# Second layer's feed-forward input projection by seven block products instead of eight (Strassen's method), its sums on GpSimd

## The chip, the cores and the metric

The kernel runs on one core of a Trainium2 chip. A core has five engines with an instruction queue each: TensorE (PE, matrix products, with its weight loads as PEld), VectorE (DVE), ScalarE (ACT), GpSimd (POOL) and SyncE (SP, which issues DMAs here). Each engine runs its own list in a fixed order, and engines wait for each other by semaphores. SBUF is the on-chip memory of 128 partitions, PSUM the accumulators of TensorE in eight banks. The metric is device time in microseconds of one execution: before, the median of three runs is 2463.46 us (2461.73, 2463.46, 2464.15).

## The reference, cut to what matters

A step of a two-layer backbone on 640 tokens (128 context tokens, 512 latent tokens), model width 1024, feed-forward width 2816. Each layer has mixers (convolution, recurrence, attention), an output projection with a gated residual, and then the feed-forward part, which is what is changed, in layer index 1 alone:

```
def trunk_layer(x, cvec, l, rope, ctx, params):
    ...
    x = x + g1 * (m @ w_out[l])
    h2 = rmsnorm(x, norm2[l]) * (1 + sc2) + sh2
    gu = h2 @ w_ffn_in[l]                       # 1024 -> 2 * 2816
    ff = jax.nn.silu(gu[..., :D_FF]) * gu[..., D_FF:]
    x = x + g2 * (ff @ w_ffn_out[l])
```

Everything is float32. `sc2`, `sh2`, `g2` come from the conditioning and differ between context and latent tokens.

## The kernel before, in words

Activations lie transposed: channels on the 128 partitions (1024 channels are 8 chunks `k`), the 640 tokens in the columns. TensorE takes float32 products as three passes of a shorter form (`fp32r`): each operand is a high part plus a low part, and a product is hi·hi + hi·lo + lo·hi. So `gemm` (its matmul is L301) makes one 128-row tile of an output with 8 k × 3 matmuls for each of two token halves, `HALF` = 256 and 384 columns: 48 matmuls a tile.

**Weights.** `panel8` brings a panel of 128 × 2048 raw float32 into one of two `rawt` buffers (one DMA of 1024 KB); for the feed-forward input (`wfi`) it holds 8 k × (128 gate columns | 128 up columns). `split_cols` makes the two parts of a tile in the ring `wR` (three slots of 1024 columns, high and low): L271 on ScalarE casts the high part, L272 on VectorE subtracts it from the raw weights for the low part.

**Activations.** Before the feed-forward part `accumulate_last` runs the last output projection of the layer with both token halves apart: first half of all eight tiles, then second half. Behind each half `after` calls `make_h`, which needs the token sums of squares of that half (`SqSum`, L504 and L505), their reciprocal root (a chain of small VectorE operations, L337 to L354), and then makes `hR_f` chunk by chunk: L521 on VectorE, L522 on ScalarE (high part), L523 on VectorE (low part).

**Feed-forward.** 22 panels stand in groups `FF_GROUPS` of 4, 2, 4, 4, 4, 4. A panel is two tiles, gate and up: 96 matmuls. The gate's eviction (`ev_silu2`) is L611 on ScalarE (tanh) and L612 on VectorE; the up tile is multiplied in by L1398 on VectorE, and `split_act` (L287 on ScalarE, L288 on VectorE) puts the high and low part into `oR`. Behind each group `accumulate` runs the output projection of that group's channels (`wfo`, matmuls L301 on `oR`) and adds into `xt` with L1187 on VectorE. The first two panels of the first group run with their first token halves ahead of their second ones (`run_tiles(jobs[:2], True)`), so that the second half of `make_h` has time.

**What sets the order.** A scheduler lays down each engine's list before the run from priorities: an instruction gets a running number, and instructions in `hp()` one that is 20000 smaller, so that they go as early as their inputs allow. Loads, splits of weights and evictions are in `hp()`. GpSimd does nothing but memsets.

Of the kernel before, what the change touches and what calls it, by code (L numbers as in the profile page):

```python
# [39 lines left out]
class Arena:  # L40
# [58 lines left out]
def tile_trunk_step(  # L99
# [55 lines left out]
    class Scope:  # L155


        def __init__(self, name, side):
            self.stack = ExitStack()
            self.name = name  # L160
            self.pool = self.stack.enter_context(tc.tile_pool(name=name, bufs=1, side=side, reuse_waits="tile"))
# [65 lines left out]
    def hp():  # L227
        return prio(20000)
# [32 lines left out]
    def split_cols(raw3):  # L261

        K, c = raw3.shape[1], raw3.shape[2]
        if wx:
            parts = [r.ap[:, : K * c] for r in wx.pop()]
        else:
            ctr["wr"] += 1
            parts = [wR[:, ctr["wr"] % NW, i, : K * c] for i in range(2)]
        hi, lo = [x.rearrange("p (k c) -> p k c", k=K) for x in parts]
        with hp():  # L270
            S.copy(hi, raw3)  # L271
            V.tensor_tensor(out=lo, in0=raw3, in1=f32(hi), op=ALU.subtract)  # L272
        return [(hi[:, k], lo[:, k]) for k in range(K)]
# [16 lines left out]
    def sub(wk, c):  # L290
        return [(h[:, c * P : (c + 1) * P], l[:, c * P : (c + 1) * P]) for h, l in wk]

    def gemm(wk, ak, hf):

        sl = HALF[hf]
# [49 lines left out]
    def stat_rstd(s, sl, scale, eps, post=None, ring=None):  # L345


        pair = (ring or wring).next()
        n = (sl.stop - sl.start) // P
        for i in range(n):  # L350
            T.matmul(pair[:, 0, i * 64 : (i + 1) * 64], lhsT=s[:, sl.start + i * P : sl.start + (i + 1) * P], rhs=ones[:, :64], start=True, stop=True)  # L351
        var = small(n)
        src = pair[:, 0, : n * 64].rearrange("p (i e) -> p i e", e=64)[:, :, 0]
        V.tensor_scalar(out=var, in0=src, scalar1=scale, scalar2=eps, op0=ALU.mult, op1=ALU.add)  # L354
        r = small(n)
        rsqrt(r, var, n)
# [123 lines left out]
    def open_h(name):  # L480
        sc = Scope(name, "left")
        hR = sc.tile([P, 2, KD, NT], F32R, "hR")
        h_act[:] = [(hR[:, 0, k, :], hR[:, 1, k, :]) for k in range(KD)]
        return sc
# [4 lines left out]
        return sc  # L489

    class SqSum:
        def __init__(self, ring, s):
            self.s = s
            self.n = [0, 0]
            self.ring = ring

        def add(self, src, hf):
            sl = HALF[hf]
            n = sl.stop - sl.start
            if self.n[hf] == 0:  # L500
                S.activation(self.s[:, sl], src[:, sl], AF.Square)
            else:
                sq = self.ring()
                S.activation(sq[:, :n], src[:, sl], AF.Square)  # L504
                V.tensor_tensor(out=self.s[:, sl], in0=self.s[:, sl], in1=sq[:, :n], op=ALU.add)  # L505
            self.n[hf] += 1

    def make_h(xs, sq, l, which, hf):

        sc = modd[l][:, 0 if which == 0 else 2]  # L510
        sh = modt[l][:, 0:8] if which == 0 else modt[l][:, 24:32]
        sl = HALF[hf]
        with hp():
            pb = stat_rstd(sq.s, sl, 1.0 / 1024, 1e-6)
        for j in range(KD):
            t = next_t()[:, : sl.stop - sl.start]
            hi, lo = h_act[j]
            for s, ss in streams(sl):
                tt = t[:, ss.start - sl.start : ss.stop - sl.start]
                pp = pb[:, ss.start - sl.start : ss.stop - sl.start]  # L520
                V.scalar_tensor_tensor(out=tt, in0=xs[j][:, ss], scalar=sc[:, j, s : s + 1], in1=pp, op0=ALU.mult, op1=ALU.mult)  # L521
                S.activation(hi[:, ss], tt, AF.Identity, bias=sh[:, j, s : s + 1])  # L522
                last = V.scalar_tensor_tensor(out=lo[:, ss], in0=tt, scalar=sh[:, j, s : s + 1], in1=f32(hi[:, ss]), op0=ALU.add, op1=ALU.subtract)  # L523
        return last
# [595 lines left out]
    def acts(lst):  # L1120
        return [(hi.ap, lo.ap) for hi, lo in lst]
# [76 lines left out]
                if j % every == every - 1:  # L1198
                    behind(last, other, 1)

    def accumulate_last(load, ak, xs, g, after):

        with four_slots():
            tiles = load(0) + load(1)
            for hf in range(2):
                for j, wk in enumerate(tiles):
                    ps, sl = gemm(wk, ak, hf)
# [35 lines left out]
    for l in range(DEPTH):  # L1243
# [77 lines left out]
        left = open_h(f"f{l}")  # L1321
# [12 lines left out]
        def out_panel(k, n):  # L1334
            return lambda pn: panel_wide(wout[l, :, k : k + n, 512 * pn : 512 * (pn + 1)], n)
# [26 lines left out]
        accumulate_last(out_panel(4, 4), acts([mh[j] for j in range(4, 8)]), xr, G1, after)  # L1362
        free_all([mh[j] for j in range(4, 8)])
        ssq.free()

        mods = iter(())
        if l + 1 < DEPTH:
# [156 lines left out]
```

## Time and profile before

| | |
|---|---|
| median of three runs | 2463.46 us |
| the profiled execution, whole | 2464.25 us |
| its span, first to last instruction | 2462.3 us |
| TensorE busy | 2429.8 us (99%) |
| VectorE busy | 1741.5 us (71%) |
| ScalarE busy | 911.1 us (37%) |
| GpSimd busy | 3.2 us |
| granted TensorE clock, mean | 0.995 |

The span is the time in which the profile saw instructions, and the whole execution is 1.95 us longer. An engine's busy time is the sum over its instructions. Lines (L301) are those of the kernel's code; "out<-in" are the program's names. A group of matmuls in the timeline carries the shape of its first one.

### The profile page before, as it was taken

What the parts mean: (1) busy time and instruction counts of PE and PEld (TensorE: products, weight loads), DVE (VectorE), ACT (ScalarE), POOL (GpSimd) and SP (SyncE); (2) the same over time, 40 slices, a digit from 0 to 9 for tenths busy, and PEclk for the clock granted to TensorE, in tenths of its full rate; (3) what the DMA queues carried; (4) which work ended last, traced back from release to release, by engine and by line L of the source; (5) the groups of instructions that cost most, each with busy time, mean ns of one, the idle gap of its engine ahead of it and who ended that gap; (6) DMA issues with size and microseconds to landing.
All of it is one profiled execution on the core that took longest, in us unless ns stands there. A gap on an engine that the chain in (4) does not pass through costs nothing.

```text
span 2462.3 us, 41375 instructions
## 1 busy us (share of the span) xinstructions
PE 2429.8 (99%) x17054; PEld 2374.3 (96%) x17054; DVE 1741.5 (71%) x3570; ACT 911.1 (37%) x1741; POOL 3.2 (0%) x36
## 2 busy tenths in 40 slices
PE   6999999999999999999999999999999999999999
PEld 4999999899999999999999999999999999999999
DVE  8588898676768897767785879977566874444343
ACT  6244664544323412222242446644333241222221
POOL 0000000000000000000000000000000000000000
PEclk8999999999999999999999999999999999999999
DMA  7122212333252244334332221121222412212121
GB/s 275 66 81 103 84 52 83 132 115 124 76 182 93 103 172 159 132 136 155 127 116 71 99 93 69 52 71 67 82 87 62 163 67 69 86 69 86 69 77 69
DMA packets 60493, 251.01 MB, mean 102 GB/s; under 512 B 6416, under 2 KB 18448, under 8 KB 37776
## 3 DMA queue, kind: packets, MB, share of 16 engines
q1 hardware_dynamic: 60304, 248.37, 28.9%
q8 instruction: 134, 2.20, 0.4%
q14 instruction: 55, 0.45, 0.1%
HBM read 230.52 MB, written 17.83 MB: 101 GB/s over the span
## 4 chain that ended last, share of the span: by engine, by line
PE 92%; DVE 5%; ACT 1%; issue 1%; DMA 0%; SPq 0%; DVEq 0%; ACTq 0%
PE psum L301 74%; PE psum L312 8%; PE psum L823 3%; PE psum L402 1%; PE psum L1074 1%; DVE aF_b L684 1%; DVE wR L272 1%; DVE small L1044 1%; PE psum L864 1%; PE psum L1066 1%; PE psum L1037 1%; PE psum L1038 1%; ACT wR L271 0%; PE psum L879 0%; PE psum L351 0%
## 5 line engine op out<-in xcount | busy, mean ns | idle before, releaser
L301 PE MATMUL psum<-hR_a,wR 128*128 128x256 f32 (+1 forms) x4512 | 705.3, 312 | 0.0
L301 PEld LDWEIGHTS psum<-hR_a,wR 128*128 128x128 f32 x4512 | 666.0, 189 | 3.0 <-issue 0.2
L271 ACT CAST wR<-rawt 128x1024 fp32r<-128x1024 f32 x316 | 329.8, 1049 | 796.9 <-PE psum L301 761.5
L272 DVE TENSOR_TENSOR wR<-rawt,wR 128x1024 fp32r<-128x1024 f32 x316 | 384.9, 1222 | 324.3 <-ACT wR L271 323.5
L301 PE MATMUL psum<-hR_f,wR 128*128 128x256 f32 (+1 forms) x4128 | 609.7, 309 | 0.0
L301 PEld LDWEIGHTS psum<-hR_f,wR 128*128 128x128 f32 x4128 | 604.1, 188 | 0.0
L301 PE MATMUL psum<-oR,wR 128*128 128x384 f32 (+1 forms) x3840 | 584.6, 311 | 4.1 <-DVE xt_x L1187 3.7
L301 PEld LDWEIGHTS psum<-oR,wR 128*128 128x128 f32 x3840 | 566.8, 190 | 8.0 <-DVE xt_x L1187 5.1
L1187 DVE SCALAR_TENSOR_TENSOR xt_x<-psum,modd,xt_x 128x128 f32<-128x128 f32 (+1 forms) x432 | 173.5, 436 | 109.7 <-PE psum L301 102.5
L312 PE MATMUL psum<-wR,hR_a 128*128 128x256 f32 x1920 | 235.2, 281 | 0.0
L312 PEld LDWEIGHTS psum<-wR,hR_a 128*128 128x128 f32 x1920 | 228.6, 188 | 0.7
L684 DVE SCALAR_TENSOR_TENSOR aF_b<-aF_b,pk 128x655 f32<-128x655 f32 x240 | 214.9, 895 | 2.8
L444 DVE CUSTOM_DVE_ANT_0 aF_m<-aF_m 128x1024 f32<-128x1024 f32 x112 | 136.7, 1220 | 0.8
L1398 DVE TENSOR_TENSOR ur<-ur,psum 128x256 f32<-128x256 f32 (+1 forms) x88 | 42.9, 488 | 74.9 <-PE psum L301 74.7
L287 ACT CAST oR<-ur 128x256 fp32r<-128x256 f32 (+2 forms) x96 | 45.8, 479 | 89.8 <-DVE ur L1398 81.3
L611 ACT ACTIVATE ur<-psum 128x256 f32<-128x256 f32 (+1 forms) x104 | 45.3, 435 | 75.4 <-PE psum L301 75.4
L1044 DVE TENSOR_REDUCE small<-psum 128x1 f32<-128x640 f32 (+1 forms) x80 | 55.1, 710 | 24.1 <-PE psum L1038 20.8
L823 PE MATMUL psum<-aF_b 128*128 128x128 f32 x500 | 70.4, 289 | 0.1
L823 PEld LDWEIGHTS psum<-aF_b 128*128 128x128 f32 x500 | 64.6, 192 | 3.7 <-issue 0.7
L811 ACT COPY aF_b<-aF_b 128x640 f32<-128x640 f32 x50 | 39.4, 787 | 75.8 <-DVE aF_b L827 40.8
L1047 ACT ACTIVATE aX<-psum,small 128x640 f32<-128x640 f32 (+1 forms) x80 | 56.5, 710 | 23.3 <-DVE small L1045 23.2
L612 DVE SCALAR_TENSOR_TENSOR ur<-ur,psum 128x256 f32<-128x256 f32 (+1 forms) x104 | 50.3, 484 | 19.2 <-ACT ur L611 19.1
(200 smaller groups left out, 2005.1 us busy)
## 6 DMA issues: line engine op xcount, KB each, us to landing
rawt<-in_win_dram SPq DMA_DIRECT2D x64, 1024.0 KB, 4.8
rawt<-in_wfi_dram SPq DMA_DIRECT2D x44, 1024.0 KB, 4.7
aF_m<-in_wmodT_dram SPq DMA_DIRECT2D x28, 1024.0 KB, 4.8
rawt<-in_wfo_dram SPq DMA_DIRECT2D x20, 1024.0 KB, 4.9
rawt<-in_wmod_dram SPq DMA_DIRECT2D x12, 1024.0 KB, 4.8
rawt<-in_wbr_dram SPq DMA_DIRECT2D x24, 512.0 KB, 3.3
aF_b<-in_wmod_dram SPq DMA_DIRECT2D x8, 1024.0 KB, 9.9
gd<-ur SPq DMA_DIRECT2D x16, 320.0 KB, 2.1
```

The lines of the kernel that those rows point to most:

```text
L271: S.copy(hi, raw3)
L272: V.tensor_tensor(out=lo, in0=raw3, in1=f32(hi), op=ALU.subtract)
L287: S.copy(hi, src)
L301: T.matmul(ps, lhsT=w, rhs=a[:, sl], start=k == 0 and q == 0, stop=k == n - 1 and q == 2)
L312: T.matmul(ps, lhsT=a[:, sl], rhs=w, start=k == 0 and q == 0, stop=k == n - 1 and q == 2)
L444: V.tensor_tensor_reduce(out=out, in0=w[:, q * 1024 : (q + 1) * 1024], in1=cb[s], scale=1.0, scalar=0.0, op0=ALU.mult, op1=ALU.add, accum_ ...
L612: V.scalar_tensor_tensor(out=dst[:, sl], in0=dst[:, sl], scalar=1.0, in1=ps, op0=ALU.add, op1=ALU.mult)
L684: V.scalar_tensor_tensor(out=accs[j], in0=pads[j][:, t : t + CO], scalar=w(j, t), in1=accs[j], op0=ALU.mult, op1=ALU.add)
L823: T.matmul(ps[:, c // 4, (c % 4) * P : (c % 4 + 1) * P], lhsT=kc[:, c * P : (c + 1) * P], rhs=qm[:, c * nc1 : (c + 1) * nc1], start=True, ...
L1044: V.tensor_reduce(out=mx[:, c : c + 1], in_=srcs[c], axis=AX.XY, op=ALU.max)
L1047: S.activation(e.rearrange("p (h n) -> p h n", h=2 if i else 1), srcs[c], AF.Exp, bias=mx[:, c : c + 1], scale=0.125, accum_out=sm[:, c : ...
L1187: last = V.scalar_tensor_tensor(out=x[:, ss], in0=ps[:, ss.start - sl.start : ss.stop - sl.start], scalar=g[:, s : s + 1], in1=x[:, ss], o ...
```

## The change

In layer 1 (`SEVEN`) the feed-forward input projection of a panel is a product of a 2 × 2 block matrix of weights (channels 0–511 and 512–1023; gate and up) with a 2 × 2 block matrix of activations (channels 0–511 and 512–1023; tokens 0–319 and 320–639). Strassen's method, in the form with fewer sums, makes it of seven block products of 512 channels × 128 rows × 320 tokens, each of 4 k × 3 = 12 matmuls. The seven products take four weight sums (L720 of the new kernel, 128 × 512, GpSimd), four activation sums (L577, L581 on VectorE, L579, L583 on GpSimd) and sums of the outputs (L762, L769 on GpSimd, L768, L773, L774, L781, L783, L732 on VectorE). Each product has its own high and low part of weights (`split_cols`, L280 and L281 now, of 512 columns; the ring holds six half slots) and of activations (`hS`, seven of them, made by the new `make_h7`: L559 on VectorE and L561 on ScalarE for the activation, L296 and L297 for its parts). The last output projection ahead of it takes the token halves as 384 and then 256 (`HALF_F`). Two sets of four banks alternate between panels. The new matmul is L728.

```diff
         else:
-            ctr["wr"] += 1
-            parts = [wR[:, ctr["wr"] % NW, i, : K * c] for i in range(2)]
+            n = 1 if K * c <= QW else 2
+            i = -(-ctr["wr"] // n) * n
+            ctr["wr"] = i + n
+            o = i % 2 * QW
+            parts = [wR[:, i // 2 % NW, q, o : o + K * c] for q in range(2)]
...
+    def make_h7(xs, sq, l, pbs, hb, hf):
...
+        def h(j, dst):
+            cuts = ((0, 0, P), (1, P, QT)) if hf == 0 else ((1, QT, 384), (1, 384, NT))
+            t0 = cuts[0][1]
+            for s, a, b in cuts:
+                pp = pbs[0][:, a:b] if b <= 384 else pbs[1][:, a - 384 : b - 384]
+                V.scalar_tensor_tensor(out=dst[:, a - t0 : b - t0], in0=xs[j][:, a:b], scalar=sc[:, j, s : s + 1], in1=pp, op0=ALU.mult, op1=ALU.mult)
+            for s, a, b in cuts if hf == 0 else ((1, QT, NT),):
+                S.activation(dst[:, a - t0 : b - t0], dst[:, a - t0 : b - t0], AF.Identity, bias=sh[:, j, s : s + 1])
+
+        def put(q, k, src):
+            split_act(src, *h_seven[q][k])
+
+        if hf == 0:
+            for j in range(KD):
+                h(j, hb[j])
+                put(j // 4, j % 4, hb[j])
+            return
+        for k in range(4):
+            t = next_t()
+            b12, b22 = t[:, :QT], t[:, QT:]
+            h(k, b12)
+            h(k + 4, b22)
+            t3, t1 = [next_u()[:, :QT] for _ in range(2)]
+            V.tensor_tensor(out=t3, in0=b22, in1=b12, op=ALU.subtract)
+            put(3, k, t3)
+            G.tensor_tensor(out=t1, in0=b12, in1=hb[k], op=ALU.subtract)
+            put(4, k, t1)
+            V.tensor_tensor(out=t3, in0=t3, in1=hb[k], op=ALU.add)
+            put(5, k, t3)
+            G.tensor_tensor(out=t1, in0=hb[k + 4], in1=t3, op=ALU.subtract)
+            put(6, k, t1)
+            put(2, k, b22)
...
+    def seven_g(src, dst, bank):
...
+        raw = load_raw(src, RAW).rearrange("p (k c) -> p k c", k=KD)
+        a11, a12, a21, a22 = raw[:, 0:4, :P], raw[:, 4:8, :P], raw[:, 0:4, P:], raw[:, 4:8, P:]
+
+        def wsum(x, y, op):
...
+            with hp():
+                G.tensor_tensor(out=v, in0=x, in1=y, op=op)
+            return r, v
+
+        def prod(ps, w, q, first):
+            wk = split_cols(w)
+            for k in range(4):
+                (wh, wl), (ah, al) = wk[k], h_seven[q][k]
+                for i, (x, y) in enumerate(((wh, ah), (wh, al), (wl, ah))):
+                    T.matmul(ps, lhsT=x, rhs=y, start=first and k == 0 and i == 0, stop=k == 3 and i == 2, skip_group_check=not first)
...
+        prod(a, a11, 0, True)
+        p1 = next_q()
+        with hp():
+            S.copy(p1, a)
+        yield
+        prod(a, a12, 1, False)
+        g0 = next_q()
+        with hp():
+            silu2(g0, a)
+        yield
+        r3, s3 = wsum(a11, a21, ALU.subtract)
+        prod(d, s3, 3, True)
...
+            S.copy(p7, d)
...
+        r1, s1 = wsum(a21, a22, ALU.add)
+        r2, s2 = wsum(s1, a11, ALU.subtract)
+        prod(c, s1, 4, True)
...
+            S.copy(p5, c)
+            G.tensor_tensor(out=p5, in0=p5, in1=p7, op=ALU.add)
...
+        r4, s4 = wsum(a12, s2, ALU.subtract)
+        prod(b, s2, 5, True)
...
+            V.tensor_tensor(out=p1, in0=b, in1=p1, op=ALU.add)
+            G.tensor_tensor(out=p5, in0=p5, in1=p1, op=ALU.add)
...
+        prod(d, a22, 6, False)
+        with hp():
+            V.tensor_tensor(out=p7, in0=d, in1=p1, op=ALU.add)
+            V.tensor_tensor(out=g0, in0=g0, in1=p7, op=ALU.mult)
+        put(g0, 0)
...
+        prod(c, s4, 2, False)
...
+            V.tensor_tensor(out=p1, in0=c, in1=p1, op=ALU.add)
+            silu2(g1, p1)
+            V.tensor_tensor(out=g1, in0=g1, in1=p5, op=ALU.mult)
+        put(g1, 1)
...
-        sq = SqSum(next_u, ssq.ap)
+        halves = HALF_F if seven else HALF
+        sq = SqSum(next_u, ssq.ap, halves)
...
+            elif seven:
+                make_h7(xr, sq, l, pbs, hb, hf)
...
-            if gi == 0:
+            if seven:
+                sets = ((0, 1, 2, 3), (4, 5, 7, 6))
+                gens = []
+                for job in jobs:
+                    gens.append(seven_g(*job, sets[ctr["bank"] % 2]))
+                    ctr["bank"] += 1
+                if gi == 0:
+                    for n in (1, 1, 5):
+                        for g in gens[:2]:
+                            take(g, n)
+                for g in gens:
+                    drain(g)
```

Three places of the instruction lists (line numbers of the kernel that each list is of). First VectorE at the start of layer 1's feed-forward part, where the second token half is made: before, two operations of 384 columns for each of eight chunks (`xt_x_17725` are the residual's tokens, `hR_f_17729` the activations' parts):

```order
L521 SCALAR_TENSOR_TENSOR ur<-xt_x_17725,modd_79,psum 128x384
L523 SCALAR_TENSOR_TENSOR hR_f_17729<-ur,modt_77,hR_f_17729 128x384
L288 TENSOR_TENSOR oR<-ur,oR 128x256
L523 SCALAR_TENSOR_TENSOR hR_f_17729<-ur,modt_77,hR_f_17729 128x384
L521 SCALAR_TENSOR_TENSOR ur<-xt_x_17725,modd_79,psum 128x384 x2
L288 TENSOR_TENSOR oR<-ur,oR 128x256
L523 SCALAR_TENSOR_TENSOR hR_f_17729<-ur,modt_77,hR_f_17729 128x384 x2
```

The same place now (`hS_f_17729` are the seven activations' parts, `aX` holds the first half's activations and the weight sums):

```order
L559 SCALAR_TENSOR_TENSOR ur<-xt_x_17725,modd_79,psum 128x64
L281 TENSOR_TENSOR wR<-aX,wR 128x512
L297 TENSOR_TENSOR hS_f_17729<-ur,hS_f_17729 128x320
L577 TENSOR_TENSOR ur<-ur 128x320
L297 TENSOR_TENSOR hS_f_17729<-ur,hS_f_17729 128x320 x3
L559 SCALAR_TENSOR_TENSOR ur<-xt_x_17725,modd_79,psum 128x256
L581 TENSOR_TENSOR ur<-ur,aX 128x320
L559 SCALAR_TENSOR_TENSOR ur<-xt_x_17725,modd_79,psum 128x64
L559 SCALAR_TENSOR_TENSOR ur<-xt_x_17725,modd_79,psum 128x256
```

For each of four `k` there are now four L559, L577, L581 and five L297. Second, ScalarE in the middle of a later group. Before, the casts of whole tiles stand between the evictions:

```order
L611 ACTIVATE ur<-psum 128x256
L271 CAST wR<-rawt 128x1024
L611 ACTIVATE ur<-psum 128x384
L287 CAST oR<-ur 128x256
L271 CAST wR<-rawt 128x1024
L287 CAST oR<-ur 128x384
```

Now (`aX` a weight sum; L741 copies product 1 out of its bank, on which product 2 is then added):

```order
L280 CAST wR<-aX 128x512
L741 COPY ur<-psum 128x320
L280 CAST wR<-rawt 128x512
L731 ACTIVATE ur<-psum 128x320
L280 CAST wR<-rawt 128x512
L753 COPY ur<-psum 128x320
L280 CAST wR<-aX 128x512
L761 COPY ur<-psum 128x320
```

The casts are of half the length and more in number, and a copy that TensorE waits for stands right behind one of them. Third, GpSimd at the same start of the feed-forward part, where before there was nothing behind the memsets at the kernel's beginning. Now the sums of weights (`aX<-rawt`) and of activations share its list:

```order
L720 TENSOR_TENSOR aX<-rawt 128x512 x2
L720 TENSOR_TENSOR aX<-aX,rawt 128x512
L579 TENSOR_TENSOR ur<-ur,aX 128x320
L583 TENSOR_TENSOR ur<-aX,ur 128x320
L579 TENSOR_TENSOR ur<-ur,aX 128x320
L720 TENSOR_TENSOR aX<-rawt,aX 128x512
L583 TENSOR_TENSOR ur<-aX,ur 128x320
L720 TENSOR_TENSOR aX<-rawt 128x512
L579 TENSOR_TENSOR ur<-ur,aX 128x320
```

So the activations' sums of the second half, on which products 4 and 6 rest, alternate with sums of weights.

## Rows read from the trace of the kernel before

**Rows 1.** The page: busy time of each engine, and the chain that ended last.
```profile
PE 2429.8 (99%) x17054; PEld 2374.3 (96%) x17054; DVE 1741.5 (71%) x3570; ACT 911.1 (37%) x1741; POOL 3.2 (0%) x36
PE 92%; DVE 5%; ACT 1%; issue 1%; DMA 0%; SPq 0%; DVEq 0%; ACTq 0%
```

**Rows 2.** TensorE's waits from 1990 us to the end: waiting, us in total, times, longest.
```profile
PE psum L301 <- ACT oR L287: 0.2, 1, 0.2
```

**Rows 3.** TensorE's timeline, layer 1's feed-forward: start us, us, line, tile, count.
```profile
1993.55 0.28 PE L301 MATMUL psum<-hR_f,wR 128*128 128x256 f32 x1
...
2050.82 28.41 PE L301 MATMUL psum<-oR,wR 128*128 128x256 f32 x192
...
2206.06 56.18 PE L301 MATMUL psum<-hR_f,wR 128*128 128x256 f32 x384
2262.07 28.38 PE L301 MATMUL psum<-oR,wR 128*128 128x256 f32 x192
...
2433.40 8.80 PE L301 MATMUL psum<-oR,wR 128*128 128x256 f32 x72
2442.04 4.33 PE L301 MATMUL psum<-oR 128*128 128x384 f32 x24
2446.20 12.64 PE L301 MATMUL psum<-oR,wR 128*128 128x384 f32 x72
```

**Rows 4.** Stretches, columns as named: start of feed-forward, one later group, its output projection.
```profile
core 0: us, PE busy (x) PEld busy (x) DVE busy (x) ACT busy (x) POOL busy (x), PEclk, DMA share, GB/s
1993.40:2014.00 20.60, 20.60 (x153) 20.36 (x152) 19.64 (x58) 11.36 (x26) 0.00 (x0) 1.00 0.29 103
...
2206.00:2262.00 56.00, 56.00 (x386) 56.00 (x385) 20.42 (x31) 14.36 (x23) 0.00 (x0) 1.00 0.22 76
2262.00:2290.30 28.30, 28.30 (x195) 28.24 (x194) 14.77 (x29) 4.61 (x5) 0.00 (x0) 1.00 0.22 76
```

**Rows 5.** VectorE by line and shape, whole run: count, busy us, mean ns, idle before.
```profile
L272 DVE TENSOR_TENSOR wR<-rawt,wR 128x1024 fp32r<-128x1024 f32 x316 | 384.9, 1222 | 324.3 <-ACT wR L271 323.5
L827 DVE TENSOR_TENSOR aF_b<-aF_b 128x320 f32<-128x320 f32 x112 | 50.1, 486 | 6.1 <-ACT aF_b L811 4.0 <-PE psum L823 1.4 <-ACT ur L729 0.3
L521 DVE SCALAR_TENSOR_TENSOR ur<-xt_x,modd,psum 128x128 f32<-128x128 f32 x48 | 15.4, 342 | 0.0
L521 DVE SCALAR_TENSOR_TENSOR ur<-xt_x,modd,psum 128x384 f32<-128x384 f32 x24 | 14.3, 612 | 0.3
L960 DVE TENSOR_TENSOR aX<-aX,ur 128x512 f32<-128x512 f32 x16 | 11.0, 689 | 0.3
L354 DVE TENSOR_SCALAR small<-psum 128x3 f32<-128x3 f32 x6 | 1.0, 160 | 1.6 <-PE psum L351 1.3
```

**Rows 6.** VectorE's timeline, three operations in a row at the start of feed-forward.
```profile
2011.28 1.15 DVE L523 SCALAR_TENSOR_TENSOR hR_f<-ur,modt,hR_f 128x384 fp32r<-128x384 f32 x2
2012.34 1.14 DVE L521 SCALAR_TENSOR_TENSOR ur<-xt_x,modd,psum 128x384 f32<-128x384 f32 x2
```

**Rows 7.** Early in the run: stretches in which TensorE waits for activations, columns as in rows 4.
```profile
44.20:50.00 5.80, 4.70 (x22) 4.50 (x23) 5.80 (x20) 2.47 (x8) 0.00 (x0) 0.58 0.91 350
50.00:60.00 10.00, 10.00 (x79) 10.00 (x79) 7.20 (x21) 3.98 (x11) 0.23 (x4) 0.90 0.19 58
```

**Rows 8.** ScalarE by line and shape, whole run.
```profile
L271 ACT CAST wR<-rawt 128x1024 fp32r<-128x1024 f32 x316 | 329.8, 1049 | 796.9 <-PE psum L301 761.5 <-PE psum L312 14.8 <-DMA xt_x<-in_xT_dram 11.8
L611 ACT ACTIVATE ur<-psum 128x384 f32<-128x384 f32 x52 | 25.2, 485 | 3.6 <-PE psum L301 3.6
L287 ACT CAST oR<-ur 128x384 fp32r<-128x384 f32 x44 | 22.4, 508 | 1.0 <-DVE ur L1398 0.9
L611 ACT ACTIVATE ur<-psum 128x256 f32<-128x256 f32 x52 | 20.0, 385 | 71.9 <-PE psum L301 71.9
```

**Rows 9.** GpSimd by line and shape, whole run.
```profile
L1275 POOL MEMSET oR<- 64x128 f32 x8 | 1.6, 199 | 1201.9 <-DVE xt_x L1187 1184.5 <-PE psum L301 17.0
L652 POOL MEMSET aF_b<- 128x15 f32 x24 | 1.4, 118 | 82.8 <-DVE masks L1237 30.1 <-PE psum L351 25.3 <-DVE ur L521 18.2
```

More of the change, by code (lines that the diff above doesn't have):

```diff
@@ L23 @@
 HALF = (slice(0, 256), slice(256, 640))
+HALF_F = (slice(0, 384), slice(384, 640))
+QT = NT // 2
+QW = 512
+SEVEN = (1,)
 FF_GROUPS = (4, 2, 4, 4, 4, 4)
@@ L213, in banks @@
             mring.use(singles(3))
-    ctr = {"raw": 0, "wr": 0, "u": 0, "t": 0}
+    ctr = {"raw": 0, "wr": 0, "u": 0, "t": 0, "q": 0, "bank": 0}
     tc.cur_priority = 1000000
@@ L291, in sub, with gemm @@
         return [(h[:, c * P : (c + 1) * P], l[:, c * P : (c + 1) * P]) for h, l in wk]
-    def gemm(wk, ak, hf):
-        sl = HALF[hf]
+    def gemm(wk, ak, hf, halves=HALF):
+        sl = halves[hf]
         ps = gring.next()[:, : sl.stop - sl.start]
@@ L491, in tile_trunk_step, with __init__ @@
     class SqSum:
-        def __init__(self, ring, s):
+        def __init__(self, ring, s, halves=HALF):
             self.s = s
@@ L495, in __init__ @@
             self.ring = ring
+            self.halves = halves
         def add(self, src, hf):
-            sl = HALF[hf]
+            sl = self.halves[hf]
             n = sl.stop - sl.start
@@ L524, in make_h, with open_hs @@
         return last
+    def open_hs(name):
+        sc = Scope(name, "left")
+        hS = sc.tile([P, 7, 2, 4, QT], F32R, "hS")
+        h_seven[:] = [[(hS[:, q, 0, k], hS[:, q, 1, k]) for k in range(4)] for q in range(7)]
+        return sc
+    h_seven = []
+    def make_h7(xs, sq, l, pbs, hb, hf):
+        sc = modd[l][:, 2]
+        sh = modt[l][:, 24:32]
+        with hp():
+            pbs.append(stat_rstd(sq.s, HALF_F[hf], 1.0 / 1024, 1e-6))
+        def h(j, dst):
[28 more added lines that the diff above has]
+            put(2, k, b22)
     def layer_params(l):
@@ L640, in pan8, with next_q, silu2, put @@
         return lambda: panel8(src)
+    def next_q():
+        ctr["q"] += 1
+        i = ctr["q"] % 10
+        return ur[:, i // 2, i % 2 * QT : (i % 2 + 1) * QT]
+    def seven_g(src, dst, bank):
+        hi, lo = [r.ap for r in dst]
+        a, b, c, d = [psum[:, i, :QT] for i in bank]
+        raw = load_raw(src, RAW).rearrange("p (k c) -> p k c", k=KD)
+        a11, a12, a21, a22 = raw[:, 0:4, :P], raw[:, 4:8, :P], raw[:, 0:4, P:], raw[:, 4:8, P:]
+        def wsum(x, y, op):
+            r = ax.alloc(QW)
+            v = r.ap.rearrange("p (k c) -> p k c", k=4)
+            with hp():
[7 more added lines that the diff above has]
+                    T.matmul(ps, lhsT=x, rhs=y, start=first and k == 0 and i == 0, stop=k == 3 and i == 2, skip_group_check=not first)
+        def silu2(t, src):
+            S.activation(t, src, AF.Tanh, scale=0.5)
+            V.scalar_tensor_tensor(out=t, in0=t, scalar=1.0, in1=src, op0=ALU.add, op1=ALU.mult)
+        def put(t, n):
+            sl = slice(n * QT, (n + 1) * QT)
+            return split_act(t, hi[:, sl], lo[:, sl])
+        prod(a, a11, 0, True)
[10 more added lines that the diff above has]
+        prod(d, s3, 3, True)
+        r3.free()
+        p7 = next_q()
+        with hp():
+            S.copy(p7, d)
+        yield
+        r1, s1 = wsum(a21, a22, ALU.add)
+        r2, s2 = wsum(s1, a11, ALU.subtract)
+        prod(c, s1, 4, True)
+        r1.free()
+        p5 = next_q()
+        with hp():
+            S.copy(p5, c)
+            G.tensor_tensor(out=p5, in0=p5, in1=p7, op=ALU.add)
+        yield
+        r4, s4 = wsum(a12, s2, ALU.subtract)
+        prod(b, s2, 5, True)
+        r2.free()
+        with hp():
+            V.tensor_tensor(out=p1, in0=b, in1=p1, op=ALU.add)
+            G.tensor_tensor(out=p5, in0=p5, in1=p1, op=ALU.add)
+        yield
+        prod(d, a22, 6, False)
+        with hp():
+            V.tensor_tensor(out=p7, in0=d, in1=p1, op=ALU.add)
+            V.tensor_tensor(out=g0, in0=g0, in1=p7, op=ALU.mult)
+        put(g0, 0)
+        yield
+        prod(c, s4, 2, False)
+        r4.free()
+        g1 = next_q()
+        with hp():
+            V.tensor_tensor(out=p1, in0=c, in1=p1, op=ALU.add)
+            silu2(g1, p1)
+            V.tensor_tensor(out=g1, in0=g1, in1=p5, op=ALU.mult)
+        put(g1, 1)
+        yield
@@ L1199, in accumulate, with accumulate_last @@
                     behind(last, other, 1)
-    def accumulate_last(load, ak, xs, g, after):
+    def accumulate_last(load, ak, xs, g, after, halves=HALF):
         with four_slots():
@@ L1206, in accumulate_last @@
                 for j, wk in enumerate(tiles):
-                    ps, sl = gemm(wk, ak, hf)
+                    ps, sl = gemm(wk, ak, hf, halves)
                     residual(ps, xs[j], g[:, j], sl)
@@ L1320, in tile_trunk_step @@
         xr = [xt[:, j] for j in range(KD)]
-        left = open_h(f"f{l}")
+        seven = l in SEVEN
+        left = (open_hs if seven else open_h)(f"f{l}")
         for j in range(KD):
@@ L1352, in tile_trunk_step @@
         ssq = ax.alloc(NT)
-        sq = SqSum(next_u, ssq.ap)
+        halves = HALF_F if seven else HALF
+        sq = SqSum(next_u, ssq.ap, halves)
+        if seven:
+            hbr = ax.alloc(4 * NT)
+            hb = [hbr.ap[:, j * QT : (j + 1) * QT] for j in range(KD)]
+            pbs = []
         def after(j, hf):
@@ L1358, in after @@
                     sq.add(xr[j], hf)
+            elif seven:
+                make_h7(xr, sq, l, pbs, hb, hf)
             else:
                 make_h(xr, sq, l, 1, hf)
-        accumulate_last(out_panel(4, 4), acts([mh[j] for j in range(4, 8)]), xr, G1, after)
+        accumulate_last(out_panel(4, 4), acts([mh[j] for j in range(4, 8)]), xr, G1, after, halves)
         free_all([mh[j] for j in range(4, 8)])
         ssq.free()
+        if seven:
+            hbr.free()
         mods = iter(())
@@ L1391, in tile_trunk_step @@
                 lo = ao.alloc(NT)
+                if seven:
+                    jobs.append((wfi[l, f], (hi, lo)))
+                    ffs.append((hi, lo))
+                    f += 1
+                    continue
                 def evs(hi=hi, lo=lo):
@@ L1405, in tile_trunk_step @@
                 f += 1
-            if gi == 0:
+            if seven:
+                sets = ((0, 1, 2, 3), (4, 5, 7, 6))
[9 more added lines that the diff above has]
+                    drain(g)
+                gring.use([psum[:, i] for i in sets[ctr["bank"] % 2]])
+                ctr["bank"] += 1
+                jobs = []
+            elif gi == 0:
                 run_tiles(jobs[:2], True)
```

## The prediction

> **What bounds the kernel now.** I read the page first: TensorE is busy for 99% of the span and holds 92% of the chain that ended last [rows 1]. Next its waits over all of layer 1's feed-forward part, from 1990 us to the end: one wait, 0.2 us [rows 2]. So this stage is TensorE's alone, and time there is matmuls taken out or waits put in. The timeline gives the price of a matmul: a group of four panels runs from 2206.06 to 2262.07 us, 56.01 us for 384 matmuls or 145.9 ns each, 14.0 us a panel [rows 3]. By columns: 72 matmuls of 256 start at 2433.40 and the next ones at 2442.04 (120 ns), 24 of 384 take until 2446.20 (173 ns) [rows 3]; on the line between, 320 columns take 146.5 ns, so a new matmul costs what an old one costs on average. The first group takes 57.27 us (1993.55 to 2050.82), 1.3 us more than a later one: that is what its start costs now [rows 3]. Last the stretches, for the room that the other engines have: in a later group VectorE is busy 20.42 of 56 us and ScalarE 14.36; in the output projection behind it 14.77 and 4.61 of 28.3. But in the first 20.6 us of the feed-forward part VectorE is busy for 19.64 [rows 4]. There it makes the second token half while TensorE has the first halves of two panels to run, and the cover is only just enough.
>
> **Removed.** A panel falls from 96 to 84 matmuls. Over 22 panels 264 go; by 145.9 ns that is 38.5 us, the whole gain there is. A panel then takes 12.26 us.
>
> **The start of the feed-forward part.** This is the largest cost. Call T0 the end of the last output projection (some 1993 us). After it TensorE can run product 1 of two panels (24 matmuls) and product 2 of the first (12), which use the first token half alone. The other five products use the second half in each of their four k, and TensorE's fixed list puts products 3, 4 and 5 (9 matmuls per k) behind these. Until the last k is made it can thus run at most 24 + 12 + 27 = 63 matmuls, 9.2 us.
>
> When is the last k made? VectorE's list says what it must do first. Its pieces: 128x320 with two SBUF inputs 486 ns, 128x512 689 ns, the scaling L521 342 ns for 128 columns and 612 for 384, so 0.21, 0.41 and 0.48 for 64, 192 and 256; small ones 0.16 [rows 5]. Two operations in a row take 0.09 less than their sum (1.14 us for two of 0.61) [rows 6]. VectorE reaches the statistics of the second half some 2.7 us past T0: the last tile's residual and square sum, then TensorE's sum. What remains of the first half stands interleaved behind it: 14 scalings (7 × 0.34 + 7 × 0.41 = 5.3), 7 low parts (3.4), 13 small ones (2.1), 2 weight parts (1.4): 12.2, less 36 × 0.09, is 9 us. Then the second half down to product 4's part for the last k: 16 scalings (8 × 0.21 + 8 × 0.48 = 5.5), 7 sums and 18 low parts of 486 ns (12.2), one weight part and one eviction (1.2): 18.9, less 43 × 0.09, is 15 us. ScalarE casts a high part ahead of each low part and GpSimd makes two of the sums per k; I add 3 us for waits on them. That is T0 + 29.7. Less the 9.2 us TensorE idles 20.5 us; less the 1.3 of before it loses 19. Bounds: if the pieces overlap better and ScalarE and GpSimd never hold VectorE, 14; if each of the 18 low parts waits half of its 0.49 for its cast, 28.
>
> **The clock after it.** Where TensorE trickled early in the run (4.70 us of matmuls in 5.8 us) its granted clock was 0.58, close to the lower level of 1.2 GHz, and in the 10 us behind that 0.90 [rows 7]. A start with 20 us of gaps should look like this: 10 us at 0.90 lose 1 us, and some 2 us of matmuls at the end of the gaps, run at 0.58, take 1.5 more. +2.5 (0 to 5).
>
> **Weight sums and casts in the steady panel.** VectorE per panel: 7 low weight parts of 0.69 and 9 operations of 320 columns by 0.486, 9.2 us of 12.26; before, 20.42 us for four panels [rows 4, 5]. ScalarE: 7 casts of 512 columns (some 0.55 from the 1049 ns of 1024), and 7 evictions and parts by 0.45 [rows 8]: 7.0 us. Both are beside TensorE. GpSimd has no two-input operation in the trace. From below it can't well beat VectorE (0.69 and 0.49 us). Its memsets cost 118 ns for 15 columns and 199 for 128 (the latter on half the partitions) [rows 9], 0.72 ns a column; with two streams read and one written instead of one written, three times that, 512 columns make 1.2 us and 320 columns 0.8. I take these, which lie nearer to the memsets than to VectorE: 4 × 1.2 + 2 × 0.8 = 6.4 us per panel, and four times VectorE's price (2.8 and 2.0 us, 15 us a panel) as the far end, which would make GpSimd the bound. In the output projection that follows each group GpSimd is free and sums of the next two panels can be made ahead, as far as raw buffers and half slots go.
>
> The new wait: product 2 is added onto product 1's bank, so it waits until ScalarE has copied that bank (L741). Between them stand seven matmuls of product 4: 1.02 us. The copy is about 0.45 us, with a hand-over of 0.2, and one cast of 0.55 can stand ahead of it: 0.65 to 1.2. I take 0.1 us per panel, +2 (0 to 4). Behind it nothing is queued on ScalarE that TensorE needs sooner than this.
>
> At the end of a group TensorE needs the last panel's activation parts some 3 us after its last product; the first matmuls of the output projection use the group's other panels, which covers 4 us. Together with weights that come late once behind the start I take +3 (1 to 6).
>
> **Sum.** −38.5 + 19 + 2.5 + 2 + 3 = −12. The profiled execution is 2464.25 us, span 2462.3 and 1.95 around it; from it 2452.3, and the median of the runs lies 0.8 lower. I say 2452.5: the profiled execution and the median differ by less than the terms are known.
>
> The trace before shows no GpSimd operation beside VectorE work: with 3.2 us of memsets [rows 1] it can't show whether the two disturb each other, and the sum above has them independent. The Trainium skill, SBUF — State Buffer, § Who interferes with whom, has a rule against this change: a VectorE instruction with two SBUF inputs and a GpSimd instruction that reads SBUF use one port pair that is locked, so the later one waits for the whole of the other. No run here shows it. By it the time is that of the second or third rival below. The skill's GPSIMD Engine Reference, on its measured `tensor_tensor` times, gives 4497 ns for 2048 float32 columns on GpSimd, as an estimate 1.1 us for 512 and 0.7 for 320; by it the sum would not move.
>
> **Rivals.**
> *A larger gain.* The start is hidden better than I think: list order is not time, and TensorE may still have 63 matmuls when VectorE is 6 to 10 us further on. A start cost of 8 instead of 19 gives 2441. Against it: 19.64 of 20.6 us of VectorE already before [rows 4], and the new half has more operations.
>
> *No gain.* VectorE and GpSimd hold each other up at the start alone. In the second half's stretch GpSimd has 7 weight sums and 8 activation sums, 14.8 us, and VectorE 25 operations with two SBUF inputs, 12.2 us, less their overlap 10; one after the other they take 25 us where I count 18 with waits. +7 there, and 0.2 per panel in the steady state (+4): 2463.5.
>
> *Slower.* They hold each other up in every panel. Two-input operations of VectorE (7 × 0.69 + 5 × 0.486 = 7.3) and GpSimd's 6.4 make 13.7 us, against 12.26 of matmuls. Where nothing is made ahead a panel takes 13.7 and 1.45 × 22 = 32 us are lost; with the start's +7, 2491. Where half of the sums are made in the output projections, +16 and +7: 2475. It decides from a panel of about 12.6 us on: with +7 at the start 8.5 us more make it slower than before by 0.2%, 0.39 a panel. The same place and price come from a GpSimd that is twice as slow as I count, with no lock. For it: 13.7 is above 12.26, and sums stand right ahead of the casts that feed TensorE. Against: VectorE and GpSimd have 28.3 us with little else behind each group [rows 4].
>
> **How the numbers follow.** A measurement of this kernel tells about 0.2% from no change: below 2458.5 is faster, above 2468.4 slower. Chances: my forecast (2446 to 2458) 0.45, the larger gain 0.11, no gain 0.21, slower 0.23. Faster 0.56, same 0.21, slower 0.23. The forecast's own range is 2444 to 2459; for 8 in 10 it must take in no gain and the milder of the slower cases, up to 2478, and below it leaves out only a start that is almost free: 2439.
>
> **What would show it.** The matmuls of L728 take 12.3 us per panel in undisturbed stretches; if a panel takes over 12.6, the waits of TensorE must name weight parts (L280, L281) and behind these GpSimd's L720. At the start TensorE idles some 20 us, waiting for parts L296 and L297, with VectorE busy throughout; if it idles less than 10, the count of VectorE's work is wrong. GpSimd's 128x512 at 1.2 us, with a mean that doesn't grow beside VectorE, and VectorE's 128x512 parts still at 0.69, clear the lock; one of them far above says it is real. TensorE's waits for L741 in sum are 2 us. The forecast is wrong if the start costs under 10 or over 28 us, or if GpSimd is on the chain that ended last in the later groups.

## The result, and the profile after

The changed kernel takes 2503.98 us (median of four runs, 2502.25 to 2505.95), the kernel before 2463.69 beside it: a ratio of 1.0168, interval 1.0156 to 1.018. It is 40 us slower, and 51 us above the forecast; the top of the range was 2478. The profiled execution took 2505.95 us, its span 2504.2.

The page of the changed kernel, as in [rows 1]:

```profile
PE 2424.8 (97%) x16790; PEld 2354.0 (94%) x16790; DVE 1877.3 (75%) x3766; ACT 990.6 (40%) x1945; POOL 185.6 (7%) x176
PE 84%; DVE 7%; ACT 3%; issue 2%; POOL 2%; DMA 2%; SPq 0%; ACTq 0%; POOLq 0%; DVEq 0%
```

TensorE's share of the chain fell from 92 to 84%, and POOL stands on it, which the forecast named as a sign that it is wrong. TensorE's two longest waits from 1990 us to the end, where [rows 2] had one of 0.2 us (waited for, us in total, times, longest of them):

```profile
PE psum L728 <- ACT ur L741: 24.0, 10, 4.8
PE psum L728 <- ACT hS_f L296: 12.1, 9, 3.3
```

The forecast had looked for such waits at the weight parts (L280, L281), not at L741. TensorE's timeline at the start, and in one later group with its output projection (compare [rows 3]):

```profile
1992.12 0.39 PE L728 MATMUL psum<-hS_f,wR 128*128 128x320 f32 x1 [1.14 <-DVE xt_x L1332]
...
2057.63 24.78 PE L728 MATMUL psum<-hS_f,wR 128*128 128x320 f32 x149 [4.85 <-ACT ur L741]
2082.25 4.30 PE L310 MATMUL psum<-oR,wR 128*128 128x256 f32 x29
...
2244.83 15.44 PE L728 MATMUL psum<-hS_f,wR 128*128 128x320 f32 x103
2262.35 12.59 PE L728 MATMUL psum<-hS_f,wR 128*128 128x320 f32 x84 [2.09 <-ACT ur L741]
2277.39 23.86 PE L728 MATMUL psum<-hS_f,wR 128*128 128x320 f32 x149 [2.45 <-ACT ur L741]
2301.10 4.29 PE L310 MATMUL psum<-oR,wR 128*128 128x256 f32 x29
...
2330.74 15.44 PE L728 MATMUL psum<-hS_f,wR 128*128 128x320 f32 x103
```

The first group takes 90.13 us (1992.12 to 2082.25), against 57.27 before. But the later ones don't gain either: from 2244.83 to 2301.10 are 56.27 us for 336 matmuls, where 384 took 56.01, and the output projection behind takes 29.64 in place of 28.3. So about a third of the surprise lies in the first group, and the rest in every group behind it. There are two stops of 2.1 and 2.5 us in this group, and its last 149 matmuls run at 159 ns each. The stretches of that group say why (columns as in [rows 4]):

```profile
2262.35:2274.90 12.55, 12.55 (x84) 12.32 (x84) 8.28 (x12) 4.44 (x9) 8.00 (x6) 1.00 0.23 85
2277.39:2301.10 23.71, 23.70 (x150) 23.50 (x150) 14.67 (x25) 10.59 (x20) 4.19 (x4) 0.93 0.26 90
```

The granted clock behind the second stop is 0.93 on average, which is about 1.7 us of 23.7: two stops of 4.5 us in sum cost some 6. In finer stretches it is 0.50 (the level of 1.2 GHz) from 2279 to 2281 us, 0.87 to 2283 and 1.00 (2.4 GHz) from there on; behind the first stop it stayed at 1.00.

What holds TensorE is named L741, ScalarE's copy of a bank. The copy itself is not slow (0.42 us); the list ahead of it is late. The chain that ended last, over the first stop:

```profile
2246.39 4.68 DMA rawt<-in_wfi_dram
...
2252.46 1.75 POOL aX L720
...
2255.86 1.34 POOL ur L762
...
2257.22 0.49 DVE ur L773
...
2258.92 1.18 DVE ur L774
...
2260.12 0.02 ACT oR L296
...
2261.47 0.51 ACT wR L280
2261.97 0.33 ACT ur L741
...
2262.35 11.58 PE psum L728 x77
```

Read it downwards: three weight sums of one panel stand in GpSimd's list ahead of L762, an eviction of another; L773 on VectorE waits for it, L774 follows and takes 1.18 us for 320 columns, and ScalarE's list holds L296, which needs L774, ahead of the cast and the copy that TensorE waits for. So lateness on GpSimd reaches TensorE through three fixed lists. Whether GpSimd is just late, or makes VectorE slow too, is in VectorE's rows from 1993 us on, by shape (count, busy us, mean ns):

```profile
L281 DVE TENSOR_TENSOR wR<-aX,wR 128x512 fp32r<-128x512 f32 x86 | 81.0, 942 | 30.7 <-ACT wR L280 28.8 <-PE psum L310 0.8
L774 DVE TENSOR_TENSOR ur<-ur 128x320 f32<-128x320 f32 x22 | 16.5, 751 | 0.2
L297 DVE TENSOR_TENSOR hS_f<-ur,hS_f 128x320 fp32r<-128x320 f32 x20 | 15.5, 804 | 0.9 <-ACT hS_f L296 0.9
L768 DVE TENSOR_TENSOR ur<-psum,ur 128x320 f32<-128x320 f32 x22 | 10.8, 489 | 11.3 <-PE psum L728 11.2
L297 DVE TENSOR_TENSOR hS_f<-aX,hS_f 128x320 fp32r<-128x320 f32 x8 | 3.9, 490 | 0.0
```

The same operation (L297) of the same size takes 490 ns while the first token half is made and GpSimd hardly works, and 804 in the second half, among GpSimd's sums. L774 reads two operands in SBUF: 751. L768 reads one in PSUM: 489. Single operations show the same: while one GpSimd sum runs, L768 (one input in PSUM) takes 0.48 us, and the L281 behind it (two in SBUF) 1.38:

```profile
2254.28 1.62 POOL L720 TENSOR_TENSOR aX<-aX,rawt 128x512 f32<-128x512 f32 x1
2254.68 0.48 DVE L768 TENSOR_TENSOR ur<-psum,ur 128x320 f32<-128x320 f32 x1
2255.08 1.38 DVE L281 TENSOR_TENSOR wR<-aX,wR 128x512 fp32r<-128x512 f32 x1
```

GpSimd's own rows:

```profile
L720 POOL TENSOR_TENSOR aX<-rawt 128x512 f32<-128x512 f32 x44 | 65.5, 1508 | 809.2 <-DMA rawt<-in_wfi_dram 800.8 <-DVE wR L281 7.0 <-DVE ur L581 1.4
L762 POOL TENSOR_TENSOR ur<-ur 128x320 f32<-128x320 f32 x22 | 23.2, 1057 | 116.7 <-ACT ur L761 116.7
```

The shortest single ones in the timeline take 1.27 and 0.86 us; these means are 1.51 and 1.06. So both engines are longer.

### The profile page after: what moved, and what is told of

It reads as the page before. It is cut to its first block, busy times and chain, and to the rows that moved or that the text cites. A ratio compares the mean times of both kernels' runs of the same rounds, so it can differ in the third digit from the quotient of the medians.

```text
span 2504.2 us, 41590 instructions
## 1 busy us (share of the span) xinstructions
PE 2424.8 (97%) x16790; PEld 2354.0 (94%) x16790; DVE 1877.3 (75%) x3766; ACT 990.6 (40%) x1945; POOL 185.6 (7%) x176
## 3 DMA queue, kind: packets, MB, share of 16 engines
q1 hardware_dynamic: 60304, 248.37, 28.3%
## 4 chain that ended last, share of the span: by engine, by line
PE 84%; DVE 7%; ACT 3%; issue 2%; POOL 2%; DMA 2%; SPq 0%; ACTq 0%; POOLq 0%; DVEq 0%
PE psum L310 59%; PE psum L321 8%; PE psum L728 6%; PE psum L968 3%; DVE wR L281 2%; PE psum L411 1%; PE psum L1219 1%; DMA rawt<-in_wfi_dram 1%; ACT wR L280 1%; POOL aX L720 1%; DVE aF_b L829 1%; PE psum L1211 1%; PE psum L1182 1%; PE psum L1009 1%; PE psum L1183 1%
## 5 line engine op out<-in xcount | busy, mean ns | idle before, releaser
L281 DVE TENSOR_TENSOR wR<-rawt,wR 128x1024 fp32r<-128x1024 f32 (+1 forms) x339 | 386.2, 1143 | 267.9 <-ACT wR L280 262.2
L280 ACT CAST wR<-rawt 128x1024 fp32r<-128x1024 f32 (+1 forms) x339 | 325.4, 965 | 623.0 <-PE psum L310 568.9
L728 PE MATMUL psum<-hS_f,wR 128*128 128x320 f32 x1848 | 302.0, 325 | 38.9 <-ACT ur L741 24.0
L728 PEld LDWEIGHTS psum<-hS_f,wR 128*128 128x128 f32 x1848 | 288.4, 198 | 51.4 <-ACT ur L741 29.0
L310 PE MATMUL psum<-hR_f,wR 128*128 128x384 f32 (+1 forms) x2064 | 304.8, 308 | 0.0
L310 PEld LDWEIGHTS psum<-hR_f,wR 128*128 128x128 f32 x2064 | 302.0, 188 | 0.0
L1332 DVE SCALAR_TENSOR_TENSOR xt_x<-psum,modd,xt_x 128x128 f32<-128x128 f32 (+2 forms) x432 | 173.0, 435 | 86.4 <-PE psum L310 79.4
L720 POOL TENSOR_TENSOR aX<-rawt 128x512 f32<-128x512 f32 x44 | 65.5, 1508 | 809.2 <-DMA rawt<-in_wfi_dram 800.8
L281 DVE TENSOR_TENSOR wR<-aX,wR 128x512 fp32r<-128x512 f32 x88 | 82.4, 936 | 30.8 <-ACT wR L280 28.8
L280 ACT CAST wR<-aX 128x512 fp32r<-128x512 f32 x88 | 54.4, 620 | 111.5 <-PE psum L310 58.8
L296 ACT CAST oR<-ur 128x320 fp32r<-128x320 f32 (+3 forms) x96 | 45.9, 481 | 130.4 <-DVE ur L774 59.6
```

Of the source, the lines that this page charges most:

```text
L720: G.tensor_tensor(out=v, in0=x, in1=y, op=op)
L728: T.matmul(ps, lhsT=x, rhs=y, start=first and k == 0 and i == 0, stop=k == 3 and i == 2, skip_group_check=not first)
L1332: last = V.scalar_tensor_tensor(out=x[:, ss], in0=ps[:, ss.start - sl.start : ss.stop - sl.start], scalar=g[:, s : s + 1], in1=x[:, ss], o ...
```

## The experiments

Two theories. **Hold-up:** a GpSimd sum and a VectorE operation with two SBUF inputs stop each other, and so both get late. **Late sums:** GpSimd is slow and the lists pass that on, with no hold-up.

### All sums on VectorE

```diff
-                G.tensor_tensor(out=v, in0=x, in1=y, op=op)
+                V.tensor_tensor(out=v, in0=x, in1=y, op=op)
```

and the same for L579, L583, L762 and L769.

> All sums (L720, L579, L583, L762, L769) on VectorE; GpSimd does nothing in the feed-forward part. Theory 'hold-up': a GpSimd sum and a VectorE operation with two SBUF inputs stop each other; in the changed kernel VectorE's L774 (two SBUF inputs) has a mean of 751 ns, while L768 of the same size with one input in PSUM has 489. Then every 320-column operation is back at 0.49 us and every 512-column one at 0.69, although VectorE has 3.8 us more work per panel, and the time falls to 2465 to 2480 us. Rival 'late sums': the loss comes from sums that take 1.3 us on a serial engine and from fixed lists that pass their lateness on, not from a hold-up; VectorE then carries some 12 us per panel of 12.3 us, its list becomes the late one, and the time stays at 2495 to 2515 us.

Measured: 2459.96 us (ten runs; ratio to before 0.9991, 0.9981 to 1.0). 44 us of the changed kernel's time are gone, though VectorE does more work. Its rows:

```profile
L281 DVE TENSOR_TENSOR wR<-aX,wR 128x512 fp32r<-128x512 f32 x86 | 59.2, 688 | 19.5 <-ACT wR L280 17.4 <-PE psum L728 1.1 <-PE psum L310 0.4
L774 DVE TENSOR_TENSOR ur<-ur 128x320 f32<-128x320 f32 x22 | 10.7, 487 | 0.2
L297 DVE TENSOR_TENSOR hS_f<-ur,hS_f 128x320 fp32r<-128x320 f32 x20 | 9.0, 486 | 0.0
```

942 is 688 again, 751 is 487, 804 is 486. TensorE's timeline:

```profile
1991.92 0.39 PE L728 MATMUL psum<-hS_f,wR 128*128 128x320 f32 x1 [1.09 <-DVE xt_x L1332]
...
2026.23 43.84 PE L728 MATMUL psum<-hS_f,wR 128*128 128x320 f32 x273 [3.79 <-ACT hS_f L296]
2069.91 28.46 PE L310 MATMUL psum<-oR,wR 128*128 128x256 f32 x192
...
2218.90 50.12 PE L728 MATMUL psum<-hS_f,wR 128*128 128x320 f32 x336
2268.86 28.46 PE L310 MATMUL psum<-oR,wR 128*128 128x256 f32 x192
```

A later group is one piece without a wait, 49.96 us, and the output projection behind is at 28.3 again. 6 us a group are won over [rows 3]. What is left to pay is the first group: 77.99 us (1991.92 to 2069.91), 28 more than a later one. The time is below the lower end of what was expected: VectorE had more room than I gave it. Against the kernel before it is no clear change.

### GpSimd busy, but not reading

```diff
-                G.tensor_tensor(out=v, in0=x, in1=y, op=op)
+                G.tensor_tensor(out=v[:, :, :1], in0=x[:, :, :1], in1=y[:, :, :1], op=op)
+                for _ in range(3):
+                    G.memset(v, 1.0)
```

and likewise with two memsets for the 320-column sums.

> Leaves out the sums: each GpSimd sum is replaced by a sum of one column (so that every wait stays) and memsets of the whole size, three for 512 columns and two for 320, which write and do not read; GpSimd is then busy for about as long as before. Hold-up: what stops VectorE is GpSimd's reading, so VectorE's operations are back at 0.49 and 0.69 us and the time falls to 2455 to 2470 us. Late sums: GpSimd is as slow and as late as before, so the time stays at 2495 to 2508 us.

Measured: 2454.19 us (four runs, ratio 0.9969, 0.9954 to 0.9984). GpSimd was busy for longer than with the sums (206.2 us over the run, 185.6 in the changed kernel):

```profile
PE 2409.9 (98%) x16790; PEld 2343.0 (96%) x16790; DVE 1824.1 (74%) x3766; ACT 990.9 (40%) x1945; POOL 206.2 (8%) x544
```

VectorE's operations are at 691 and 488 ns, and of TensorE's waits for the copy 0.4 us remain:

```profile
L281 DVE TENSOR_TENSOR wR<-aX,wR 128x512 fp32r<-128x512 f32 x87 | 60.1, 691 | 29.2 <-ACT wR L280 27.8
L297 DVE TENSOR_TENSOR hS_f<-ur,hS_f 128x320 fp32r<-128x320 f32 x20 | 9.3, 488 | 1.2 <-ACT hS_f L296 1.0
PE psum L734 <- ACT ur L747: 0.4, 1, 0.4
```

Three memsets of 525 ns behind the one column are longer than a weight sum (1.8 us against 1.44 on average), two of 365 ns about as long as an output sum (1.0 against 1.12). The long reading is missing, and the loss is gone. One thing more differs: the scheduler laid some memsets of an output sum between those of the weight sums. Where a later group makes its third panel's sums, the output sum is done 4.4 us after the first weight sum begins, in place of 6.0 in the group above, and the fourth weight sum is done after 9.0, in place of 7.2. What the earlier output sum is worth by itself was not measured; the next run, which takes the output sums off GpSimd altogether, still takes 43 us more than this one. This run is also what the forecast described, and it came to 1.7 us from it.

### Only the output sums on VectorE

L762 and L769 alone, `G.tensor_tensor` to `V.tensor_tensor`.

> Only the two output sums per panel (L762, L769) go to VectorE; weight and activation sums stay on GpSimd. Late sums: in the later groups TensorE's waits of 2.1 to 2.6 us for L741 come from L762, which stands behind three weight sums in GpSimd's list and holds, over L773 and L774, ScalarE's list; without it these waits fall below 0.5 us and with them the low clock behind them, 5 to 6 us a group: 2478 to 2488 us. Hold-up: a quarter of GpSimd's time goes, the stretched L281 and L774 stay; 2490 to 2498 us.

Measured: 2497.21 us (two runs, ratio 1.0138, 1.0118 to 1.0159).

```profile
PE psum L728 <- ACT ur L741: 17.0, 9, 2.8
L281 DVE TENSOR_TENSOR wR<-aX,wR 128x512 fp32r<-128x512 f32 x87 | 75.7, 870 | 25.8 <-ACT wR L280 24.7
L762 DVE TENSOR_TENSOR ur<-ur 128x320 f32<-128x320 f32 x22 | 20.1, 916 | 0.1
L774 DVE TENSOR_TENSOR ur<-ur 128x320 f32<-128x320 f32 x22 | 10.7, 484 | 0.2
```

The link of the chain that I had suspected first (L762 behind weight sums on GpSimd) is gone, and TensorE still waits 17.0 us for the copy, in place of 24.0. L774 is back at 484 ns, but L281 is not, and L762, now VectorE's own operation with two SBUF inputs, takes 916 ns; with GpSimd idle it took 489 there. The time lies where the hold-up had it (2490 to 2498), 7 us below the changed kernel. Net of what the two sums now cost VectorE, that link is worth these 7 us; the other 37 of the 44 are still lost.

### Without the second token half's activations

Products 3 to 7 take the parts of the first half:

```diff
-                (wh, wl), (ah, al) = wk[k], h_seven[q][k]
+                (wh, wl), (ah, al) = wk[k], h_seven[q % 2][k]
```

and `make_h7` returns at once for the second half.

> Leaves out the second token half's activations and their sums: products 3 to 7 take the parts of the first half. The start of the feed-forward part then has nothing to wait for. If the start is what failed in the forecast, its first group falls from 88 us to some 56 as in the later groups, and the time to 2468 to 2474 us; what is then left above 2425 (2463.5 less 38.5) is the loss of the steady panels, some 40 us. If the start lost only the 19 us of the forecast and the rest is spread over all groups, the time is 2482 us or more.

Measured: 2477.75 us (three runs, 2472.81 to 2478.23), between the two expectations. The first group still takes 63.3 us, and the four later ones 55.0 to 55.8, nearly what they take in the changed kernel (55.3 to 56.5):

```profile
1990.84 0.31 PE L730 MATMUL psum<-hS_f,wR 128*128 128x320 f32 x1
...
2030.61 23.72 PE L730 MATMUL psum<-hS_f,wR 128*128 128x320 f32 x149 [4.13 <-ACT ur L743]
2054.16 4.32 PE L310 MATMUL psum<-oR,wR 128*128 128x256 f32 x29
```

So the second half's activations cost some 27 us here (90.13 less 63.3), and the 4 us stop late in the first group is not theirs: it stands ahead of the last 149 matmuls, as the second stop of a later group does. The loss lies in both places.

### The start on VectorE, the later groups on GpSimd

```diff
-                G.tensor_tensor(out=v, in0=x, in1=y, op=op)
+                (V if ctr["g0"] else G).tensor_tensor(out=v, in0=x, in1=y, op=op)
```

with `ctr["g0"]` set in the first group, the same for L762 and L769, and L579 and L583 on VectorE.

> Sums on VectorE only for the activations and in the first group; from the second group on as in the changed kernel, on GpSimd. If the hold-up adds up from its places, the first group takes the 78 us of the run with all sums on VectorE, the later ones 56 and their output projections 29.6 as in the changed kernel: 2504 less 10.5, 2490 to 2496 us. If instead the late start pushes the later groups into each other and they heal with it, 2475 us or less.

Measured: 2490.61 us (two runs, ratio 1.0114, 1.0096 to 1.0133). It is in the range of a hold-up that adds up from its places: the first group takes 79.10 us and the four later ones 55.1 to 55.8. By the medians, GpSimd's sums in the first group cost 13 us (2503.98 less 2490.61), those behind it 31 (2490.61 less 2459.96).

### All sums on VectorE, the first two panels by ordinary products

The start is left, and there VectorE is hardly ever idle (busy for 31.11 of the 33 us from 1993 us on, with all sums on it). What can be changed is how much TensorE has to do before it needs the sums. Two panels of eight products need no sum:

```diff
...
+                if gi == 0:
+                    plain_two(jobs[:2])
+                    for k in range(4):
+                        split_act(hb[k + 4], *h_seven[6][k])
+                    hbr.free()
+                    jobs = jobs[2:]
+                    ctr["bank"] += 1
...
```

`plain_two` runs gate and up tiles of both panels for tokens 0–319, then for 320–639, 24 matmuls of 320 columns each. `make_h7` makes the plain parts of the second half first and the sums behind them; the plain parts of the second half's first 512 channels lie where those of product 6 come later.

> All sums on VectorE, as in the run with all sums there (2460 us), and the first two panels of the first group by the eight ordinary products (token halves of 320, both first halves ahead), with the parts for them made before any activation sum; the seventh activation's parts wait until these two panels are through. In the run with all sums on VectorE the first group took 78 us, against 50.0 of a later one: 28 us are its start. Theory 'cover': TensorE idles there because only 63 matmuls (9.4 us) can run before the last sum; now 96 can (14.3 us) before the second half is needed, which needs 8 us of VectorE in place of 15, and the sums lie beside the second halves of the two panels. Idle falls to some 7 us, the sums come some 3 us late, 24 more matmuls cost 3.6: 13 to 15 us lost in place of 28, 2443 to 2450 us. Rival 'VectorE's sum of work': the same work must be done before the third panel, so the idle time only moves there, and the 3.6 us come on top: 2458 to 2466 us.

Measured: 2443.48 us (five runs), ratio 0.9924 (0.991 to 0.9937): 18.5 us faster than the kernel before, 60 faster than the change.

```profile
1990.13 0.61 PE L807 MATMUL psum<-hS_f,wR 128*128 128x320 f32 x3
...
2024.93 5.63 PE L729 MATMUL psum<-hS_f,wR 128*128 128x320 f32 x35
2031.47 21.61 PE L729 MATMUL psum<-hS_f,wR 128*128 128x320 f32 x133 [0.90 <-DVE wR L281]
2052.91 28.35 PE L310 MATMUL psum<-oR,wR 128*128 128x256 f32 x192
```

The first group takes 62.78 us in place of 77.99, with 24 matmuls more. The one wait in the third panel is 0.9 us: the rival, by which the idle time only moves there, falls. One more thing changes with the cover: two panels by ordinary products need no sums of weights and outputs, and VectorE is busy for 58.4 us in the first group in place of 71.1. How much of the 15 us is the cover and how much the shorter list on VectorE, this run does not separate.

## Why the prediction was wrong

**The step that failed** is the sentence that "the sum above has them independent", that is, the 1.2 and 0.8 us for GpSimd's sums as work beside other work. They are not beside: each stops VectorE's operations with two SBUF inputs, and is stopped. The mechanism stood as a rival with 0.23, and its price there was too low (2491 at most). With GpSimd busy but not reading, the changed kernel takes 2454; the reading costs some 50 us. Place by place, the changed kernel less that run: 15.9 us in the first group (90.13 less 74.24; the rival had 7 for the start), 7.1 in the second group with its projection, 5.3 to 6.7 in each of the four later groups, and some 1.2 in each of four output projections. In sum these are 52.5 us; the two profiled executions differ by 52.3.

Why more than the rival's price: in the later groups half of the weight sums were made ahead in the output projection (8 of 16 from 2301.10 to 2330.70 us), which is the rival's milder case, 16 us for 22 panels or 2.9 a group. It only added durations. It left out that a held-up L281 or L774 (1.36 and 1.17 us in the group above) also holds the lists behind it, down to ScalarE's copy, and that TensorE then runs some matmuls at the lower clock: behind one of the two stops, 149 in 23.71 us, 1.6 more than at 148.7 ns each. It also left out the projections. No run takes these parts from each other.

The hold-up as the rows show it: two SBUF inputs, 0.49 to 0.75 and 0.80 us; one in PSUM, 0.49; GpSimd writing only, no effect. That is the rule of the Trainium skill, SBUF — State Buffer, § Who interferes with whom (VectorE's second SBUF input comes through the read interface that it shares with GpSimd). The runs agree with it in all three points. I had it at hand and gave it less than the row-based sum, since no row of before could show it; but that no row shows an overlap is no evidence that it is free.

**The other terms.** The matmul: 12.26 us a panel was forecast, 49.96 / 4 = 12.49 measured where nothing waits; 148.7 ns, not 145.9, so 320 columns lie a little above the line through 256 and 384, and 22 × (14.00 − 12.49) gives back 33.2 us, not 38.5. The start: 19 and 2.5 for the clock were forecast; with GpSimd not reading, the first group is 74.24 us against 50.08 of a later one, 24.2 less the 1.3 of before: 22.9, near the 21.5. The split was off: in the first 30.9 us of that run TensorE counts as idle for 9.2, with a granted clock of 0.67, so more of the start than forecast shows as matmuls at the lower clock. With all sums on VectorE the start is 26.8. The wait for L741: 2 us forecast, 24.0 in the changed kernel, 0.9 and 0.4 without the hold-up, so without it the term was, if anything, too large. The group ends with late weights: 3 us forecast; with GpSimd not reading, TensorE waits 0.6 us for weight parts (L280) and never for `oR`. That this run came to 1.7 us from the forecast is thus in part luck: 5 us too much saving and some 4 us too much waiting nearly cancel. GpSimd's prices, 1.2 and 0.8, measured 1.27 and 0.86 at best, 1.44 and 1.12 on average. "VectorE and GpSimd have 28.3 us behind each group", the argument against the slow rival, holds for half of the panels: in the later group above the chain starts with a load that came when the group had begun (2246.39 us, the group 2244.83).

What stays open: how the 5.3 to 6.7 us of a later group split between GpSimd's own delay and VectorE's was not measured; no run slows one without the other.

## What to carry to other kernels

An idle GpSimd is not free room for VectorE's kind of work: where VectorE spends its time on operations with two SBUF inputs, as here, moving a sum to GpSimd makes both late, and the sum cost less on VectorE itself, though that was busy for 77% of the run. A product saved on TensorE is won only where its operands are ready; at a stage's start, count what can run before the last operand and put work there that needs none of the new sums. A copy that a matmul waits for takes the age of the whole list ahead of it on its engine, so read the chain above the engine that the wait names.

## What was not expected of the hardware

A VectorE operation that is held up shows as a longer operation, not as idle time: L297 went from 490 to 804 ns with an idle time near none. So a mean by shape, set against the same shape elsewhere in the trace, is the place to look. And a stop of 2 us need not be over when it ends: behind the second of two in one group the granted clock fell to 0.50 (2279 to 2281 us) and was back at 1.00 from 2283 us on; behind the first it had stayed at 1.00.
